# Hyena's long convolution on one NeuronCore: all elementwise steps between its transforms on VectorE, none on GpSimd

## The chip, the core and the metric

The kernel runs on one core of one Trainium2 chip. A core has five engines that run their own instruction streams and meet through semaphores: TensorE (PE in the profile; its weight loads are PEld), VectorE (DVE), ScalarE (ACT), GpSimd (POOL) and SyncE (SP, which here only issues DMAs). The metric is the device time of one execution in microseconds (us); lower is better.

## The reference

Two layers of a diffusion backbone over 128 context and 1024 latent tokens. Each layer projects the normed tokens into three groups that run side by side: a convolution module, attention with normed and rotated q and k, and a Hyena long convolution. Then follow an output projection and a gated FFN. The part that the change touches is the long convolution, twice per layer:

```
def _fft_conv(u, kf, bias):
    L = u.shape[1]
    U = jnp.fft.rfft(u, n=2 * L, axis=1)
    y = jnp.fft.irfft(U * kf[None], n=2 * L, axis=1)[:, :L]
    return y + u * bias
...
def _hyena(z, p):
    z = _dwconv(z, p['hy_short_w'], p['hy_short_b'])
    v, g1, g2 = jnp.split(z.astype(jnp.float32), 3, axis=-1)
    kf = _hyena_filter_fft(z.shape[1], p)
    bias = p['hy_bias'].astype(jnp.float32)
    u = _fft_conv(v, kf[:, 0], bias[0]) * g1
    u = _fft_conv(u, kf[:, 1], bias[1]) * g2
    return u.astype(z.dtype)
```

## The kernel before

All matrix work is in fp32 split into a high and a low part, so one product is three matmuls (`hh*whi`, `hl*whi`, `hh*wlo`). A layer has four phases; each is one loop, and a list scheduler puts every engine's instructions into one fixed order before the run.

Phase 1 (`phase1`) is the input projection: 16 output blocks, each of 72 matmuls (tile `win`; 2304 in both layers, 1152 in each). The weights of a block come as `wraw`; ScalarE makes the high part `whi`, GpSimd the low part `wlo`. After its matmuls a block is treated by its kind: blocks of the Hyena group go through a short convolution (`raw`, then `zs` on VectorE); q and k blocks through a norm and a rotation (TensorE sums `s` and broadcasts `nr`, VectorE's reciprocal `nsd`, its `nw` and `sh`, and GpSimd's two products with the rotary table); gates through `th`.

Between the matmuls of these blocks, the Hyena convolutions run as a background generator. `hy_conv` does one 2048-point convolution: four DFT matrix products (`ft`, read out into `ta` and `sd`), then elementwise butterflies (`e`, `p`, `o`, `abcd`, `jk`, `X`), the product with the filter's spectrum for four parts n (`W` and `Y`, from `X` and the loaded `khat`), butterflies back (`isd`, `s`, `d`, `e`, `f`, `vw`, `pqmn`, `gh`, `Z`), the split into `zh` and `zl`, and four inverse products (`iy`). The 128 context tokens take a small path of their own within it (`xp`, `pab`, `pyh`, `yp`, `yp2t`). It runs twice per layer; the second ends with transposes `y2t` and the products `hyo`, which are split into `mh` and `ml` and written to memory.

When the second convolution is done, its buffers are given to attention: keys `k` are loaded by GpSimd's DMA queue and queries `q` by SP's, and TensorE starts with the row maxima (`S`, reduced by VectorE into `mx`). Phase 2 is attention with the convolution module beside it; phases 3 and 4 are the output projection (`wo`) and the FFN (`up`, `dn`).

In `hy_conv`, `eng` is GpSimd. It does the 16 butterflies on 128x256 tiles (`abcd`, `jk`, `pqmn`, `gh`: four each) and the four 128x1024 products `W`; everything else elementwise in it is VectorE's.

Of the kernel before, what the change touches and what calls it, by code (L numbers as in the profile page):

```python
# [134 lines left out]
class Kern:  # L135
# [684 lines left out]
    def hy_conv(self, l, o, mid):  # L820

        nc = self.nc
        eng = nc.gpsimd

        def v2(x):
            return x.rearrange("p (c x) -> p c x", c=2)

        def sw(x):
            return v2(x)[:, ::-1, :]

        def v4(t):
            return t[:].rearrange("p (n x) -> p n x", n=4)

        def two(name):
            t = self.H(name)
            return t[:, 0:512], t[:, 512:1024]

        def part(F, n, r):
            t = self.T("ft")
            uh, ul = self.u[r]  # L840
            for c in range(2):
                j = 128 * (2 * n + c)
                self.mm3(t[:, 256 * c : 256 * c + 256], F[:, j : j + 128], F[:, 512 + j : 640 + j], uh, ul, True, True)
            return t

        def sd(q):
            F = self.hq.tile([128, 1024], F32R, tag="fm", name="fmat", bufs=2)
            self.const(F[:], "dftf", q)
            a = part(F, 0, q)
            m = self.M("ta")  # L850
            nc.scalar.copy(m[:], a[:])
            b = part(F, 1, q + 4)
            s, d = two("sd")
            self.add(s, m[:], b[:])
            self.sub(d, m[:], b[:])
            return s, d

        s0, d0 = sd(0)
        s2, d2 = sd(2)
        yield  # L860
        E0, E2 = two("e02")
        self.add(E0, s0, s2)
        self.sub(E2, s0, s2)
        P1, P3 = two("p13")
        self.add(v2(P1), v2(d0), sw(d2))
        self.sub(v2(P3), v2(d0), sw(d2))
        yield
        s1, d1 = sd(1)
        s3, d3 = sd(3)
        yield  # L870
        O0, O2 = two("o02")
        self.add(O0, s1, s3)
        self.sub(O2, s1, s3)
        t = self.H("abcd")
        A, C, B, D = (t[:, 256 * k : 256 * k + 256] for k in range(4))
        self.add(A, d1[:, 0:256], d1[:, 256:512], eng)
        self.sub(C, d1[:, 256:512], d1[:, 0:256], eng)
        self.sub(B, d3[:, 256:512], d3[:, 0:256], eng)
        self.add(D, d3[:, 0:256], d3[:, 256:512], eng)
        J, K_ = two("jk")  # L880
        self.add(J[:, 0:256], A, B, eng)
        self.sub(J[:, 256:512], B, A, eng)
        self.add(K_[:, 0:256], C, D, eng)
        self.sub(K_[:, 256:512], C, D, eng)
        yield
        Y = []
        for n in range(4):
            X = self.H("X")
            x = v4(X)
            if n == 0:  # L890
                self.add(x[:, 0:4:2, :], v2(E0), v2(O0))
                self.sub(x[:, 1:4:2, :], v2(E0), v2(O0))
            elif n == 1:
                self.add(x[:, 0:4:3, :], v2(E2), sw(O2))
                self.sub(x[:, 1:3, :], v2(E2), sw(O2))
            else:
                c = SQH if n == 2 else -SQH
                self.stt(x[:, 0:4:3, :], v2(J), c, v2(P1), ALU.mult, ALU.add)
                self.stt(x[:, 1:3, :], v2(K_), c, v2(P3), ALU.mult, ALU.add)
            K = self.hq.tile([128, 1024], F32, tag="kh", name="khat", bufs=2)  # L900
            nc.sync.dma_start(K[:], self.khD[l][o, n])

            def kb(c):
                return K[:, 512 * c : 512 * c + 512].unsqueeze(1).to_broadcast([128, 2, 512])

            y, w = self.H("Y"), self.H("W")
            self.mul(v2(w[:]), v2(X[:]), kb(1), eng)
            self.mul(v2(y[:]), v2(X[:]), kb(0))
            self.sub(y[:, 0:512], y[:, 0:512], w[:, 512:1024])
            self.add(y[:, 512:1024], y[:, 512:1024], w[:, 0:512])  # L910
            Y.append(y)
            yield
        mid()

        ds = []
        for n in range(2):
            s, d = two("isd")
            self.add(v2(s), v4(Y[n])[:, 0:4:2, :], v4(Y[n])[:, 1:4:2, :])
            self.sub(v2(d), v4(Y[n])[:, 0:4:2, :], v4(Y[n])[:, 1:4:2, :])
            ds.append((s, d))  # L920
        (s0, d0), (s2, d2) = ds
        S13, D13 = self.H("s13"), self.H("d13")
        self.add(S13[:], Y[2][:], Y[3][:])
        self.sub(D13[:], Y[2][:], Y[3][:])
        yield
        e0, e1 = two("e01")
        self.add(e0, s0, s2)
        self.sub(e1, s0, s2)
        f0, f1 = two("f01")
        s1, s3 = v4(S13)[:, 0:4:2, :], v4(S13)[:, 1:4:2, :]  # L930
        self.add(v2(f0), s1, s3)
        self.sub(v2(f1), s1, s3)

        V, W = two("vw")
        self.sub(v2(V), v2(d0), sw(d2))
        self.add(v2(W), v2(d0), sw(d2))
        t = self.H("pqmn")
        p_, q_, m_, n_ = (t[:, 256 * k : 256 * k + 256] for k in range(4))
        d = v4(D13)
        self.sub(p_, d[:, 0, :], d[:, 2, :], eng)  # L940
        self.add(q_, d[:, 0, :], d[:, 2, :], eng)
        self.add(m_, d[:, 1, :], d[:, 3, :], eng)
        self.sub(n_, d[:, 1, :], d[:, 3, :], eng)
        G, Hh = two("gh")
        self.sub(G[:, 0:256], p_, m_, eng)
        self.add(G[:, 256:512], p_, m_, eng)
        self.add(Hh[:, 0:256], q_, n_, eng)
        self.sub(Hh[:, 256:512], n_, q_, eng)
        yield
        for n in range(4):  # L950
            Z = self.H("Z")
            z = v4(Z)
            if n == 0:
                self.add(Z[:, 0:512], e0, f0)
                self.sub(Z[:, 512:1024], e0, f0)
            elif n == 1:

                self.add(z[:, 2:0:-1, :], v2(e1), sw(f1))
                self.sub(z[:, 0:4:3, :], v2(e1), sw(f1))
            else:  # L960
                c = SQH if n == 2 else -SQH
                self.stt(z[:, 0:4:3, :], v2(G), c, v2(V), ALU.mult, ALU.add)
                self.stt(z[:, 1:3, :], v2(Hh), c, sw(W), ALU.mult, ALU.add)
            zh, zl = self.H("zh", F32R), self.H("zl", F32R)
            self.hilo(zh[:], zl[:], Z[:])
            F = self.hq.tile([128, 1024], F32R, tag="fm", name="imat", bufs=2)
            self.const(F[:], "dfti", n)
            t = self.T("iy")
            for u in range(2):
                for c in range(2):  # L970
                    j = 2 * u + c
                    self.mm3(t[:, 256 * u : 256 * u + 256], F[:, 128 * j : 128 * j + 128], F[:, 512 + 128 * j : 640 + 128 * j],
                             zh[:, 256 * j : 256 * j + 256], zl[:, 256 * j : 256 * j + 256], c == 0, c == 1)
            yield n, t
# [896 lines left out]
```

## Time and profile before

| | |
|---|---|
| median of 3 runs | 3429.67 us (3425.01 to 3435.25) |
| the profiled execution: its time, its span | 3432.48 us, 3430.7 us |
| PE busy, share of the span | 3172.1 us, 92% |
| DVE | 2195.4 us, 64% |
| ACT | 1190.9 us, 35% |
| POOL | 725.4 us, 21% |
| mean granted clock of TensorE | 0.948 |

The time of an execution is 1.8 us more than its span, the stretch from its first instruction to its last. A busy share is a mean over phases that have different limits: what a step costs is read in its own stretch. A duration on DVE or POOL in this profile is the time from an instruction's start to its end, so a wait in the middle of one shows as a longer instruction and not as idle time. The granted clock is a share of TensorE's full 2.4 GHz.

### The profile page before, as it was taken

How to read it: one execution, taken by the hardware profiler on the slowest of the kernel's cores; microseconds unless marked ns; L12 is line 12 of the kernel's file. 1: busy time of each engine (PE TensorE's matmuls, PEld its weight loads, DVE VectorE, ACT ScalarE, POOL GpSimd, SP SyncE). 2: the span in 40 equal slices, each digit the busy share in tenths (PEclk: the TensorE clock that was granted, in tenths of full speed). 3: DMA queues.
4: the chain of work that ended last, by engine and by line, in shares of the span. 5: the costliest groups of instructions: out<-in, count | busy, mean ns of one | idle time of the engine just before them, and what ended most of it. 6: DMA issues, size and time to landing. Idle time of an engine off the chain costs nothing. (4 is left out here: it accounts for less than half of the span.)

```text
span 3430.7 us, 44677 instructions
## 1 busy us (share of the span) xinstructions
PE 3172.1 (92%) x17330; PEld 2794.1 (81%) x17330; DVE 2195.4 (64%) x3318; ACT 1190.9 (35%) x1976; POOL 725.4 (21%) x558
## 2 busy tenths in 40 slices
PE   5988878999889999999999889789999999999997
PEld 3878833458889999999998887334699999999997
DVE  7877789764764554445577795996446554455556
ACT  3422333352253222333344233334434223333323
POOL 6645444221210000000024562442101000000002
PEclk8989978999989999999999998889999999999998
DMA  7564454536311111111123535442511111111112
GB/s 285 163 206 155 129 154 140 173 114 222 122 53 41 44 42 42 44 42 42 44 70 112 163 114 157 141 148 79 191 41 37 44 44 41 44 43 41 44 42 70
DMA packets 152328, 336.09 MB, mean 98 GB/s; under 512 B 21360, under 2 KB 57844, under 8 KB 145589
## 3 DMA queue, kind: packets, MB, share of 16 engines
q1 hardware_dynamic: 147412, 318.69, 28.7%
q0 software_dynamic: 4704, 14.55, 1.5%
q8 instruction: 137, 2.24, 0.3%
q14 instruction: 75, 0.61, 0.1%
HBM read 264.86 MB, written 68.31 MB: 97 GB/s over the span
## 5 line engine op out<-in xcount | busy, mean ns | idle before, releaser
L236 PE MATMUL up<-hl,whi 128*128 128x384 f32 (+1 forms) x2112 | 713.7, 338 | 4.6 <-DVE hl L225 3.2
L236 PE MATMUL up<-hh,whi 128*128 128x384 f32 (+1 forms) x2112 | 711.7, 338 | 3.6 <-ACT hh L230 2.3
L236 PE MATMUL up<-hh,wlo 128*128 128x384 f32 (+1 forms) x2112 | 712.5, 338 | 0.0
L213 DVE TENSOR_TENSOR wlo<-wraw,whi 128x512 fp32r<-128x512 f32 x296 | 207.1, 700 | 646.5 <-ACT whi L230 644.2
L230 ACT CAST whi<-wraw 128x512 fp32r<-128x512 f32 x362 | 223.8, 618 | 845.1 <-PE dn L236 358.2
L236 PEld LDWEIGHTS up<-hl,whi 128*128 128x128 f32 x2112 | 399.5, 189 | 6.5 <-DVE hl L225 4.7
L236 PEld LDWEIGHTS up<-hh,whi 128*128 128x128 f32 x2112 | 399.5, 189 | 4.4 <-ACT hh L230 2.9
L236 PEld LDWEIGHTS up<-hh,wlo 128*128 128x128 f32 x2112 | 399.3, 189 | 0.0
L213 POOL TENSOR_TENSOR acc<-acc,sq 128x384 f32<-128x384 f32 x51 | 56.0, 1106 | 1623.4 <-ACT sq L210 1622.4
L225 DVE SCALAR_TENSOR_TENSOR xt<-dn,mod,xt 128x128 f32<-128x128 f32 (+2 forms) x704 | 332.0, 511 | 71.7 <-PE dn L236 71.5
L236 PE MATMUL dn<-gh,wlo 128*128 128x384 f32 (+1 forms) x1056 | 359.2, 340 | 0.0
L236 PE MATMUL dn<-gh,whi 128*128 128x384 f32 (+1 forms) x1056 | 358.2, 339 | 0.0
L236 PE MATMUL dn<-gl,whi 128*128 128x384 f32 (+1 forms) x1056 | 357.5, 339 | 0.0
L225 DVE SCALAR_TENSOR_TENSOR fu<-pd,vec,fu 128x1154 f32<-128x1154 f32 (+2 forms) x192 | 253.8, 1323 | 91.7 <-ACT fu L210 89.1
L236 PE MATMUL win<-hh,whi 128*128 128x384 f32 x768 | 270.4, 354 | 27.7 <-ACT raw L729 10.2
L236 PE MATMUL win<-hl,whi 128*128 128x384 f32 x768 | 269.4, 351 | 7.8 <-POOL hl L213 3.6
L236 PE MATMUL win<-hh,wlo 128*128 128x384 f32 x768 | 268.5, 350 | 1.2 <-POOL wlo L213 1.2
L1344 DVE TENSOR_REDUCE mx<-S 128x1 f32<-128x384 f32 x384 | 197.4, 547 | 66.3 <-PE S L236 65.8
L1665 ACT COPY pd<-up 128x384 f32<-128x384 f32 (+1 forms) x352 | 131.9, 401 | 237.7 <-PE up L236 237.7
L210 ACT ACTIVATE p<-st 128x1024 f32<-128x1024 f32 x144 | 147.0, 1021 | 166.9 <-PE st L236 166.5
L236 PEld LDWEIGHTS dn<-gl,whi 128*128 128x128 f32 x1056 | 200.0, 189 | 0.0
L236 PEld LDWEIGHTS S<-k,q 128*128 128x128 f32 x384 | 76.2, 218 | 151.8 <-DVE mx L1344 64.3
(295 smaller groups left out, 5675.6 us busy)
## 6 DMA issues: line engine op xcount, KB each, us to landing
wmod<-in_w_mod SPq DMA_DIRECT2D x48, 1024.0 KB
wraw<-in_w_up SPq DMA_DIRECT2D x176, 256.0 KB
wraw<-in_w_dn SPq DMA_DIRECT2D x88, 256.0 KB
wraw<-in_w_in SPq DMA_DIRECT2D x64, 256.0 KB
q<-qD SPq DMA_DIRECT2D x48, 256.0 KB
mh<-mixD SPq DMA_DIRECT2D x16, 576.0 KB
ml<-mixD SPq DMA_DIRECT2D x16, 576.0 KB
khD<-fK SPq DMA_DIRECT2D x16, 512.0 KB
```

The costliest lines, as they stand in the source:

```text
L210: return self.nc.scalar.activation(out, in_, f, **k)
L213: return (eng or self.nc.vector).tensor_tensor(out, a, b, op=op)
L225: return (eng or self.nc.vector).scalar_tensor_tensor(out, a, s, b, op0=op0, op1=op1)
L230: self.nc.scalar.copy(hi, src)
L236: self.nc.tensor.matmul(out, l, r, start=start, stop=stop)
L1344: nc.vector.tensor_reduce(m3[:, k, s : s + 1], S[:, :384], op=ALU.max, axis=AX.X)
L1665: self.nc.scalar.copy(p[:, u + o : v + o], t[:, u - a : v - a])
```

## The change

`eng` is taken out of `hy_conv`: the 20 instructions per convolution that GpSimd did are issued on VectorE, in the same program order, on the same tiles. With two convolutions in each of two layers these are 64 instructions on 128x256 and 16 on 128x1024.

```
 def hy_conv(self, l, o, mid):
-        eng = nc.gpsimd
...
-        self.add(A, d1[:, 0:256], d1[:, 256:512], eng)
-        self.sub(C, d1[:, 256:512], d1[:, 0:256], eng)
-        self.sub(B, d3[:, 256:512], d3[:, 0:256], eng)
-        self.add(D, d3[:, 0:256], d3[:, 256:512], eng)
+        self.add(A, d1[:, 0:256], d1[:, 256:512])
+        self.sub(C, d1[:, 256:512], d1[:, 0:256])
+        self.sub(B, d3[:, 256:512], d3[:, 0:256])
+        self.add(D, d3[:, 0:256], d3[:, 256:512])
...
-        self.add(J[:, 0:256], A, B, eng)
+        self.add(J[:, 0:256], A, B)
...
-            self.mul(v2(w[:]), v2(X[:]), kb(1), eng)
+            self.mul(v2(w[:]), v2(X[:]), kb(1))
...
-        self.sub(p_, d[:, 0, :], d[:, 2, :], eng)
+        self.sub(p_, d[:, 0, :], d[:, 2, :])
...
-        self.sub(G[:, 0:256], p_, m_, eng)
+        self.sub(G[:, 0:256], p_, m_)
...
```

The scheduler builds its order anew, so other instructions move too. On VectorE, in the first convolution of layer 0, these rows stood before, from the first `Y<-Y,W` (each row is an operation, its output and inputs, its size, and how many of it):

```order
L213 TENSOR_TENSOR Y<-Y,W 128x512 x2
L225 SCALAR_TENSOR_TENSOR X<-jk,p_1578 128x2x256
L225 SCALAR_TENSOR_TENSOR X<-jk,p_1578 128x512
L213 TENSOR_TENSOR Y<-Y,W 128x512 x2
L213 TENSOR_TENSOR Y<-X,khat 128x1024
L225 SCALAR_TENSOR_TENSOR X<-jk,p_1578 128x2x256
L225 SCALAR_TENSOR_TENSOR X<-jk,p_1578 128x512
L213 TENSOR_TENSOR Y<-Y,W 128x512 x2
L213 TENSOR_TENSOR Y<-X,khat 128x1024
L213 TENSOR_TENSOR pab<-xp,khatp 128x512 x2
L213 TENSOR_TENSOR Y<-Y,W 128x512 x2
L1076 RECIPROCAL nsd<-nsd 128x18
```

and these stand now, from the `zs` that comes ahead of the same `Y<-Y,W`:

```order
L225 SCALAR_TENSOR_TENSOR zs<-raw,vec_77,zs 128x1153
L213 TENSOR_TENSOR Y<-Y,W 128x512 x2
L213 TENSOR_TENSOR W<-X,khat 128x1024
L213 TENSOR_TENSOR Y<-X,khat 128x1024
L225 SCALAR_TENSOR_TENSOR X<-jk,p_1578 128x2x256
L225 SCALAR_TENSOR_TENSOR X<-jk,p_1578 128x512
L213 TENSOR_TENSOR Y<-Y,W 128x512 x2
L213 TENSOR_TENSOR W<-X,khat 128x1024
L213 TENSOR_TENSOR Y<-X,khat 128x1024
L225 SCALAR_TENSOR_TENSOR X<-jk,p_1578 128x2x256
L225 SCALAR_TENSOR_TENSOR X<-jk,p_1578 128x512
L1075 RECIPROCAL nsd<-nsd 128x18
```

`W` stands ahead of each `Y<-X,khat`, and the reciprocal `nsd` comes ahead of the third `Y<-Y,W`, where it came behind the fourth; two `zs` stand ahead of it in both orders. The same list has `abcd` and `jk` right behind `o<-sd`, some ten rows up.

On TensorE, at the end of layer 0's second convolution, the last transposes `y2t` were followed before by:

```order
L246 MATMUL y2t<-cst,y_3102 128x128 x4
L236 MATMUL win<-hh,wlo 128x384
L236 MATMUL s_3913<-cst,nsq 128x2 x9
L236 MATMUL win<-hh,whi 128x384
L236 MATMUL win<-hl,whi 128x384
L236 MATMUL win<-hh,wlo 128x384
L236 MATMUL win<-hh,whi 128x384
L236 MATMUL win<-hl,whi 128x384
```

and by 61 `win` matmuls in all ahead of the first `S`. Now there stands:

```order
L246 MATMUL y2t<-cst,y_3102 128x128 x4
L236 MATMUL nr<-cst,nsd 64x128 x6
L236 MATMUL s_4098<-cst,nsq 128x2 x9
L236 MATMUL nr<-cst,nsd 64x128 x18
L236 MATMUL sp<-kpt,qp 128x128 x2
L246 MATMUL ppt<-cst,pp 128x128 x2
L236 MATMUL avp<-ppm,vpt 64x128 x2
L236 MATMUL S<-k_3584,q_3599 128x384 x3
```

All 1152 `win` matmuls of the layer come ahead of the last `y2t`, and the last norms (`nr`, `s`) and a first piece of the context tokens' attention (`sp`, `ppt`, `avp`) ahead of `S`. In layer 1 the last `y2t` has moved back behind 73 more `win` (93 of them still follow it, where 166 did). Between `xp` and the first `yp` of layer 0's second convolution stand 203 `win`, where 157 did; of layer 1's second, 130 where 140 did. The first `iy` of layer 0 stands behind 648 of the `win`, where it stood behind 610; that of layer 1 behind 1716, where it stood behind 1668.

## Rows read from the trace of the kernel before

**Rows 1.** Busy time, granted clock and DMA of three stretches, by engine.

```profile
core 0: us, PE busy (x) PEld busy (x) DVE busy (x) ACT busy (x) POOL busy (x), PEclk, DMA share, GB/s
190.00:433.00 243.00, 205.86 (x1300) 196.99 (x1301) 192.64 (x237) 72.33 (x135) 117.82 (x104) 0.93 0.49 154
1040.00:1800.00 760.00, 757.04 (x4336) 756.40 (x4335) 408.93 (x611) 240.94 (x392) 19.55 (x18) 1.00 0.16 45
1870.00:2091.00 221.00, 194.44 (x1208) 188.25 (x1206) 170.43 (x212) 69.26 (x123) 125.70 (x94) 0.93 0.44 140
```

**Rows 2.** Timeline of TensorE: start, us, instruction, idle time before it and releaser.

```profile
248.81 1.55 PE L236 MATMUL nr<-cst,nsd 128*64 128x128 f32 x12 [11.71 <-DVE nsd L1076]
...
269.31 0.43 PE L236 MATMUL nr<-cst,nsd 128*64 128x128 f32 x2 [4.66 <-DVE nw L213]
...
346.20 0.69 PE L236 MATMUL win<-hh,whi 128*128 128x384 f32 x1 [5.68 <-ACT th L210]
...
382.35 0.33 PE L246 MATMUL yp2t<-cst,yp 128*128 128x128 f32 x1 [3.76 <-DVE hyo L213]
...
1910.92 0.69 PE L236 MATMUL win<-hh,whi 128*128 128x384 f32 x1 [10.17 <-ACT raw L729]
...
1931.30 0.39 PE L236 MATMUL iy<-zh,imat 128*128 128x256 f32 x1 [3.02 <-ACT zh L230]
...
2009.40 0.69 PE L236 MATMUL win<-hh,whi 128*128 128x384 f32 x1 [7.62 <-ACT nw L210]
```

**Rows 3.** Timeline of VectorE in layer 0's first convolution.

```profile
211.63 7.59 DVE L213 TENSOR_TENSOR o<-sd 128x512 f32<-128x512 f32 x2
...
248.68 0.68 DVE L213 TENSOR_TENSOR pab<-pab 128x256 f32<-128x256 f32 x2
```

**Rows 4.** Timeline of GpSimd at the first of these.

```profile
211.21 2.82 POOL L213 TENSOR_TENSOR abcd<-sd 128x256 f32<-128x256 f32 x4
...
216.64 1.42 POOL L213 TENSOR_TENSOR jk<-abcd 128x256 f32<-128x256 f32 x2
```

**Rows 5.** Instructions by tile, whole run: ns least/median/most, first and last start.

```profile
L213 DVE TENSOR_TENSOR Y<-Y,W x32: 674/1382/2894, 229.2 to 2021.2; 128x512 f32<-128x512 f32 x32
L213 DVE TENSOR_TENSOR Y<-X,khat x16: 1210/1346/3475, 220.5 to 2014.9; 128x1024 f32<-128x1024 f32 x16
L213 POOL TENSOR_TENSOR W<-X,khat x16: 2395/2689/3396, 220.5 to 2014.3; 128x1024 f32<-128x1024 f32 x16
L213 POOL TENSOR_TENSOR abcd<-sd x16: 726/750/1854, 211.2 to 1985.8; 128x256 f32<-128x256 f32 x16
```

**Rows 6.** GpSimd's low parts of weights, 190 to 433 us: busy, mean, idle before.

```profile
L213 POOL TENSOR_TENSOR wlo<-wraw,whi 128x512 fp32r<-128x512 f32 x21 | 32.7, 1557 | 57.3 <-ACT whi L230 57.3
```

**Rows 7.** Timeline of VectorE, layer 0's second convolution, last `sd` and `pyh`.

```profile
323.71 0.68 DVE L213 TENSOR_TENSOR sd<-ta,ft 128x512 f32<-128x512 f32 x1
...
368.53 0.68 DVE L213 TENSOR_TENSOR pyh<-pab,pyh 128x512 fp32r<-128x512 f32 x1
```

**Rows 8.** Timeline of VectorE in layer 1: first convolution, then the second.

```profile
1873.49 1.90 DVE L213 TENSOR_TENSOR o<-sd 128x512 f32<-128x512 f32 x2
...
1908.81 1.41 DVE L225 SCALAR_TENSOR_TENSOR zs<-raw,vec,zs 128x1153 f32<-128x1153 f32 x1
...
1983.51 1.28 DVE L213 TENSOR_TENSOR sd<-ta,ft 128x512 f32<-128x512 f32 x2 [2.34 <-PE ft L236]
...
2024.90 0.68 DVE L213 TENSOR_TENSOR pyh<-pab,pyh 128x512 fp32r<-128x512 f32 x1
```

**Rows 9.** TensorE's last transposes of each layer (by tile), and the first `S`.

```profile
L246 PE MATMUL y2t<-cst,y x16: 272/273/273, 391.4 to 409.5; 128*128 128x128 f32 x16
...
432.82 1.30 PE L236 MATMUL S<-k,q 128*128 128x384 f32 x3 [4.41 <-DMA q<-qD]
...
L246 PE MATMUL y2t<-cst,y x16: 270/273/473, 2047.0 to 2068.9; 128*128 128x128 f32 x16
...
2090.98 0.77 PE L236 MATMUL S<-k,q 128*128 128x384 f32 x3 [1.80 <-DMA q<-qD]
```

More of the change, by code (lines that the diff above doesn't have):

```diff
@@ L875, in hy_conv @@
         A, C, B, D = (t[:, 256 * k : 256 * k + 256] for k in range(4))
-        self.add(A, d1[:, 0:256], d1[:, 256:512], eng)
-        self.sub(C, d1[:, 256:512], d1[:, 0:256], eng)
-        self.sub(B, d3[:, 256:512], d3[:, 0:256], eng)
-        self.add(D, d3[:, 0:256], d3[:, 256:512], eng)
+        self.add(A, d1[:, 0:256], d1[:, 256:512])
+        self.sub(C, d1[:, 256:512], d1[:, 0:256])
+        self.sub(B, d3[:, 256:512], d3[:, 0:256])
+        self.add(D, d3[:, 0:256], d3[:, 256:512])
         J, K_ = two("jk")
-        self.add(J[:, 0:256], A, B, eng)
-        self.sub(J[:, 256:512], B, A, eng)
-        self.add(K_[:, 0:256], C, D, eng)
-        self.sub(K_[:, 256:512], C, D, eng)
+        self.add(J[:, 0:256], A, B)
+        self.sub(J[:, 256:512], B, A)
+        self.add(K_[:, 0:256], C, D)
+        self.sub(K_[:, 256:512], C, D)
         yield
@@ L939, in hy_conv @@
         d = v4(D13)
-        self.sub(p_, d[:, 0, :], d[:, 2, :], eng)
-        self.add(q_, d[:, 0, :], d[:, 2, :], eng)
-        self.add(m_, d[:, 1, :], d[:, 3, :], eng)
-        self.sub(n_, d[:, 1, :], d[:, 3, :], eng)
+        self.sub(p_, d[:, 0, :], d[:, 2, :])
+        self.add(q_, d[:, 0, :], d[:, 2, :])
+        self.add(m_, d[:, 1, :], d[:, 3, :])
+        self.sub(n_, d[:, 1, :], d[:, 3, :])
         G, Hh = two("gh")
-        self.sub(G[:, 0:256], p_, m_, eng)
-        self.add(G[:, 256:512], p_, m_, eng)
-        self.add(Hh[:, 0:256], q_, n_, eng)
-        self.sub(Hh[:, 256:512], n_, q_, eng)
+        self.sub(G[:, 0:256], p_, m_)
+        self.add(G[:, 256:512], p_, m_)
+        self.add(Hh[:, 0:256], q_, n_)
+        self.sub(Hh[:, 256:512], n_, q_)
         yield
```

## Prediction

> **What bounds the kernel now.** I read the busy time by stretch first. Over the FFN (1040 to 1800 us) TensorE is busy for 757 of 760 us at a granted clock of 1.00, the level of 2.4 GHz; nothing this change touches works there. The convolutions run in phase 1 of each layer, 190 to 433 us and 1870 to 2091 us, and there TensorE is idle for 37.1 and 26.6 us and its clock is 0.93 [rows 1]. VectorE is busy for 79% and 77% of these stretches. So the change is worth what it does to TensorE's waits there.
>
> Second, the timeline of TensorE, for its idle times with what ended them. The seven long ones are 11.71, 4.66, 5.68 and 3.76 us in layer 0 and 10.17, 3.02 and 7.62 us in layer 1 [rows 2], 46.6 of the 63.7 us. Each ends with VectorE or with a ScalarE step that hangs on VectorE (`raw` on the previous block's `zs`, `nw` and `th` on buffers that VectorE's rotation steps free, `zh` on `Z`).
>
> Third, the timelines of VectorE and GpSimd side by side, for why VectorE is late. Two `o<-sd` take 7.59 us from 211.63 [rows 3], where a `Y<-Y,W` of the same size can take 0.674 [rows 5]. In that time GpSimd works from 211.21 to 218.06 without a pause, `abcd` to `jk` [rows 4], and VectorE is through at 219.2, some 1.2 us later. The median `Y<-Y,W` takes 1.38 us, twice its least [rows 5]. Here one of the two stands still while the other works.
>
> The Trainium skill, "SBUF — State Buffer", section "Who interferes with whom", has this as a rule: a VectorE instruction with two inputs in SBUF contends with a GpSimd instruction that reads SBUF, the one that issued first holds the shared port for the whole instruction, and the other blocks. The trace agrees (7.59 us for work of 1.35). Taken in full it would give VectorE back all that GpSimd no longer does; that is the third rival below.
>
> **The change, part by part.** *Work.* GpSimd loses 16 `W` of 2.69 us at the median, 43.0 us, and 64 small ones of at least 0.726, 46.5 us: 89 us at least [rows 5]. VectorE gets 16 products of the form of `Y<-X,khat`, 1.21 us when nothing holds it up [rows 5], and 64 of 128x256, 0.34 each by the pair of `pab` at 0.68 [rows 3]: 19.4 + 21.8 = 41 us, 10.3 per convolution. Which of TensorE's waits this moves is worked out chain by chain. I add the instructions of the new order at their least (0.674 for 128x512, 1.21, 0.34, and 1.41 for `zs` [rows 8]; 0.5 for the small ones of the rotation, between these), and 1.56 us for each `wlo` that GpSimd still does in the stretch [rows 6], as if every one stopped VectorE.
>
> *Layer 0, first convolution.* Before, TensorE stood from 237.1 to 248.8 until the reciprocal `nsd` was done, 37.2 us after VectorE's 211.63 [rows 2, 3]. Now 14 of 128x512, 6 of 1024, 8 small ones and 2 `zs` stand ahead of it: 9.4 + 7.3 + 2.7 + 2.8 = 22.2, and two `wlo` 3.1, which is 236.9. The wait goes, and I count 11 of its 11.71 us; bounds 8.6 (both `wlo` twice as long) and 11.71. Of the next, 4.66 at `nr`, I take 2: the first `iy`, 38 `win` later in the order (6.7 us at 757.04/4336 = 0.175 each [rows 1]), becomes the place that waits for `Z`. Bounds 0 and 4.66.
>
> *Layer 0, second convolution.* From the last `sd` (ends 324.4) to `pyh` (369.2) VectorE took 44.8 us [rows 7]. The new list is 25 of 512, 8 of 1024, 10 small and 14 of the rotation, 16.9 + 9.7 + 3.4 + 7.0 = 37.0, and three `wlo`: 41.7. TensorE has 203 `win`, 35.5 us, and 2 us of `nr` to do meanwhile, so 4 us of waiting remain at `yp`, where 5.68 and the smaller ones at `yp` stood; and `yp2t`, which waited 3.76, has 29 `win` (5 us) ahead of it. I take 8 us; bounds 3 (the chain's own gain) and 9.4 (both waits).
>
> *Layer 1, first convolution.* The `zs` that freed `raw` was through at 1910.2, 36.7 us after 1873.49 [rows 8]; TensorE had stood since 1900.7 [rows 2]. Now 12 of 512, 6 of 1024, 8 small and 4 `zs` lead to it: 8.1 + 7.3 + 2.7 + 5.6 = 23.7, and two `wlo`: 1900.3. Of 10.17 us 9 go, and the 3.02 at `iy`, behind 48 more `win` (8.4 us), too: 12. Bounds 6 and 13.2.
>
> *Layer 1, second convolution.* From the end of `sd` at 1984.8 to that of `pyh` at 2025.6 it took 40.8 us [rows 8]. The new list is 16.9 + 9.7 + 3.4 + 5.0 and three `wlo`, 39.7; TensorE has 130 `win` and some 4 us of small matmuls, 27 us. The 7.62 us wait becomes one at `yp`: I take the chain's gain, 1 us. Bounds -8 and 7.6.
>
> *The tails.* Attention can start only when the last `hyo` is out. From the last `y2t` to the first `S` it took 23.3 us (409.5 to 432.8) and 22.1 us (2068.9 to 2091.0), and both ended with the load of `q` [rows 9]. In layer 0 that was covered by 61 `win` (10.7 us), which now come first; nothing covers it now but 27 `nr` and a piece of the context's attention. In layer 1 the last `y2t` comes 73 `win` (12.8 us) later. What came out of the cover is done earlier, so nothing is lost where VectorE and the loads set the pace behind `S`, and all of it where TensorE does. I take a loss of 2 us each; bounds 0 and 23.5 together.
>
> *The clock.* 0.93 against 1.00 [rows 1]: one point is worth 4.0 us of the 400 us busy in the two stretches. It fell where TensorE had stood. I take one point, 4 us; bounds 0 and 28.
>
> *What GpSimd keeps.* Its rotation products also stop VectorE, which the lists leave out: 4 us against, bounds 0 and 10.
>
> Edits that cost nothing: GpSimd's own queue gets shorter, which hides behind its waits for `whi` (57.3 us idle ahead of 21 `wlo` [rows 6]); the `khat` loads have to follow faster, but two buffers give them the 7 us that VectorE needs from one `Y<-X,khat` to the `W` two parts on (X, two `Y<-Y,W`, `W`, `Y`, X, two `Y<-Y,W`, by the prices above). If they don't land, each part waits for its load.
>
> Sum: 11 + 2 + 8 + 12 + 1 + 4 - 4 - 4 = 30 us. The profiled execution took 3432.48 us, 2.8 above the median of the runs, so 3402.5 for one like it and 3399.7 by the median: **3400 us**.
>
> **The rivals.** *No change.* The tails take it back: the chains give 14 + 3 + 10 + 1 = 28 us and the covers taken away are worth 23.5, which leaves 4.5: 3425. For it: TensorE's total work is the same, and layer 0's end stands bare. Against: in both layers the start of `S` was set by loads, not by TensorE [rows 9].
>
> *Slower.* VectorE becomes the bound: `wlo` and the rotation go on holding it, it gains no speed, and 10.3 us more lie in each of the four chains. Where half of that reaches TensorE it is 20 us, 3450; in full 41, 3471. It decides if the median `Y<-Y,W` stays above 1 us. For it: VectorE is already busy for 79% [rows 1], and the 89 us go to the busier engine. Against: the least and the median of the same instruction [rows 5]. The Trainium skill, "Perfetto Trace Analysis", section "Optimizing Scalar/DVE Operations", speaks for this side where it advises to move work off a saturated VectorE, to ScalarE or even GpSimd; the same section warns that between VectorE and GpSimd it might not help, because they share a read port, and by the rows above the trace sides with the warning.
>
> *More than forecast.* Every microsecond of GpSimd's 89 had stopped VectorE, so VectorE is relieved by 48 net, all seven waits go (46.6) and the clock gives another 8: 55, or 3375. Against: in the second convolutions the counted chains hardly get shorter.
>
> **How the numbers follow.** A difference of 0.3%, 10 us, is what a measurement here can tell from no change. Chances: the forecast (a gain of 11 to 45 us) 0.68, more than that 0.07, no change 0.13, slower 0.12. So faster 0.75, same 0.13, slower 0.12. The range runs from just beyond the third rival's 3375 to 3438, where the slower rival begins; it leaves out some 0.16. The forecast's own range is 3385 to 3419.
>
> **What would show it.** Right: `Y<-Y,W` at a median near 0.7 us and `o<-sd` at 1.3 for two; the 11.71 and the 10.17 us waits gone; a wait of some 10 us at `yp` in layer 1; some 20 us of TensorE idling between the last `y2t` and `S` in layer 0. Wrong: `Y<-Y,W` still above 1 us, `S` starting later than 432.8 us, TensorE waiting for `wlo` (held up by long runs of VectorE) or VectorE for `khat`.

## The result and the profile after

The changed kernel takes 3379.84 us, the median of four runs (3374.35 to 3384.74), where the kernel before took 3431.21 beside it: a ratio of 0.985, interval 0.9834 to 0.9865, or 51 us less. The forecast was 3400. The result lies inside the prediction's whole range (3375 to 3438), but 5 us below the forecast's own (3385 to 3419) and 5 us above the third rival's 3375.

The profiled execution has a span of 3372.2 us, the shortest of the four runs, against 3430.7; the accounts below are of this pair and add up to 58.5 us. Of these, 46.1 are TensorE's idle time (258.6 to 212.5) and 12.4 its busy time (3172.1 to 3159.7).

First the windows of each layer's convolutions, the stretch from the last `y2t` to the first `S`, and attention up to the first `wo`. Before:

```profile
core 0: us, PE busy (x) PEld busy (x) DVE busy (x) ACT busy (x) POOL busy (x), PEclk, DMA share, GB/s
190.00:409.50 219.50, 187.84 (x1165) 180.32 (x1166) 183.08 (x215) 63.85 (x118) 108.89 (x92) 0.93 0.45 145
409.50:432.80 23.30, 17.84 (x136) 16.47 (x135) 9.56 (x22) 8.47 (x17) 8.93 (x12) 0.95 0.83 238
432.80:786.30 353.50, 309.69 (x1360) 149.47 (x1360) 276.26 (x479) 144.05 (x206) 120.15 (x64) 0.88 0.46 154
...
1800.00:2068.90 268.90, 236.94 (x1440) 226.95 (x1439) 210.72 (x264) 95.59 (x176) 144.37 (x117) 0.93 0.40 128
2068.90:2090.98 22.08, 20.28 (x125) 20.22 (x123) 6.98 (x14) 8.72 (x16) 7.62 (x10) 1.00 0.77 238
2090.98:2456.90 365.92, 317.75 (x1410) 162.33 (x1410) 286.90 (x484) 148.34 (x215) 122.14 (x67) 0.88 0.40 130
```

The same stretches after (layer 1's begins again at the end of the FFN):

```profile
190.00:392.90 202.90, 196.20 (x1268) 189.31 (x1269) 173.15 (x266) 72.13 (x130) 62.54 (x55) 0.97 0.52 166
392.90:420.60 27.70, 11.15 (x80) 8.17 (x78) 15.25 (x40) 9.07 (x21) 14.61 (x21) 0.58 0.83 229
420.60:754.00 333.40, 297.91 (x1299) 142.51 (x1299) 259.99 (x448) 138.65 (x193) 109.76 (x53) 0.89 0.47 158
...
1766.10:2022.90 256.80, 244.12 (x1512) 234.40 (x1511) 203.49 (x306) 97.34 (x180) 101.25 (x81) 0.97 0.42 139
2022.90:2047.90 25.00, 22.02 (x139) 21.11 (x138) 7.47 (x17) 9.21 (x18) 5.62 (x9) 0.93 0.84 241
2047.90:2400.50 352.60, 307.93 (x1323) 150.44 (x1321) 282.67 (x478) 145.69 (x210) 120.17 (x65) 0.87 0.40 130
```

Idle time of TensorE is the length less the first busy time. In the convolutions it falls from 31.66 to 6.70 and from 31.96 to 12.68 us: 44.2 in all. In layer 0's tail it rises from 5.46 to 16.55, in layer 1's from 1.80 to 2.98: 12.3 lost. In the attention phases it falls by 8.3 and 3.5: 11.8. In layer 0's convolutions VectorE is busy for 173 us where it was for 183, with more work.

Some of the idle times of TensorE that are left there, the two longest among them (timeline of the kernel after; in brackets the idle time before the row and what ended it), against [rows 2]:

```profile
250.22 0.86 PE L236 MATMUL yp<-pyh,pmat 128*128 128x256 f32 x5 [1.37 <-DVE pyh L213]
...
353.58 0.38 PE L236 MATMUL yp<-pyh,pmat 128*128 128x256 f32 x1 [1.75 <-ACT pyh L230]
...
1970.50 0.44 PE L236 MATMUL win<-hh,whi 128*128 128x384 f32 x1 [2.90 <-DVE th L225]
...
1997.20 0.38 PE L236 MATMUL iy<-zh,imat 128*128 128x256 f32 x1 [1.04 <-ACT zh L230]
```

At none of the places of the seven long ones is more left than these 2.90 us. VectorE's timeline at the start of that first one, against [rows 3], and at the end of layer 1's second, against [rows 8]:

```profile
212.53 1.29 DVE L213 TENSOR_TENSOR o<-sd 128x512 f32<-128x512 f32 x2
213.74 1.42 DVE L213 TENSOR_TENSOR abcd<-sd 128x256 f32<-128x256 f32 x4
...
236.35 0.25 DVE L1075 RECIPROCAL nsd<-nsd 128x18 f32<-128x18 f32 x1
...
1941.65 1.29 DVE L213 TENSOR_TENSOR sd<-ta,ft 128x512 f32<-128x512 f32 x2 [1.17 <-PE vt L246]
...
1978.35 0.68 DVE L213 TENSOR_TENSOR pyh<-pab,pyh 128x512 fp32r<-128x512 f32 x1
```

Two `o<-sd` take 1.29 us where they took 7.59, and the reciprocal is through 24.1 us after their start instead of 37.2. By tile (ns least/median/most), against [rows 5]:

```profile
L213 DVE TENSOR_TENSOR Y<-Y,W x32: 621/680/1780, 225.9 to 1972.1; 128x512 f32<-128x512 f32 x32
L213 DVE TENSOR_TENSOR Y<-X,khat x16: 1208/1214/2311, 221.2 to 1967.6; 128x1024 f32<-128x1024 f32 x16
L213 DVE TENSOR_TENSOR W<-X,khat x16: 1208/1213/2034, 220.1 to 1966.4; 128x1024 f32<-128x1024 f32 x16
L213 DVE TENSOR_TENSOR abcd<-sd x16: 411/418/422, 213.7 to 1945.7; 128x256 f32<-128x256 f32 x16
```

The 80 moved instructions are busy for 51.0 us on VectorE (20.9 for `W`; 5.9, 7.1, 8.3 and 8.8 for `abcd`, `jk`, `pqmn` and `gh`), and yet its busy time falls from 2195.4 to 2166.0 us: what it had to do before takes 80 us less, nearly all of the 89 that GpSimd's work was at its least (GpSimd was busy with it for 111 us). GpSimd's own busy time falls by less than that, by 98.6 us (725.4 to 626.8): its `wlo` now take 128.1 us in all, where they took 110.5.

Attention's first rows in TensorE's timeline, against [rows 9] (`issue` is idle time in which the profile shows nothing that the engine waited for):

```profile
420.59 1.30 PE L236 MATMUL S<-k,q 128*128 128x384 f32 x3 [4.82 <-issue]
...
2047.87 0.70 PE L236 MATMUL S<-k,q 128*128 128x384 f32 x3
```

### The profile page after: what moved, and what is told of

The parts are those of the page before. It is cut to its first block, busy times and chain, and to the rows that moved or that the text cites. A ratio compares the mean times of both kernels' runs of the same rounds, so it can differ in the third digit from the quotient of the medians.

```text
span 3372.2 us, 44662 instructions
## 1 busy us (share of the span) xinstructions
PE 3159.7 (94%) x17330; PEld 2782.6 (83%) x17330; DVE 2166.0 (64%) x3398; ACT 1193.9 (35%) x1978; POOL 626.8 (19%) x478
## 4 chain that ended last, share of the span: by engine, by line
PE 72%; DVE 17%; DMA 6%; issue 2%; ACT 1%; POOL 1%; SPq 1%; DVEq 0%; ACTq 0%; POOLq 0%
PE up L236 32%; PE dn L236 16%; PE win L236 6%; PE wo L236 6%; DVE ca L225 3%; PE av L236 2%; PE st L236 2%; DVE mx L1343 2%; PE S L236 2%; DVE nt L225 1%; DMA q<-qD 1%; DVE Y L213 1%; PE fc L236 1%; DVE hl L225 1%; PE flt L236 1%
## 5 line engine op out<-in xcount | busy, mean ns | idle before, releaser
L225 DVE SCALAR_TENSOR_TENSOR xt<-dn,mod,xt 128x128 f32<-128x128 f32 (+2 forms) x704 | 332.3, 513 | 71.7 <-PE dn L236 71.5
L236 PEld LDWEIGHTS dn<-gh,whi 128*128 128x128 f32 x1056 | 199.7, 189 | 0.0
```

What stands on the lines that cost most here:

```text
L225: return (eng or self.nc.vector).scalar_tensor_tensor(out, a, s, b, op0=op0, op1=op1)
L236: self.nc.tensor.matmul(out, l, r, start=start, stop=stop)
```

## The experiments

Theory A: VectorE's instructions with two operands in SBUF stand still while GpSimd reads its own, so the work that leaves GpSimd gives VectorE its time back. Theory B: nothing stands still; GpSimd is only the slower engine in the chain (2.69 us for a `W` against 1.21), and the chain gets shorter. The table has all runs; the columns behind the interval are of the profiled execution.

| run | median, us | ratio to before, interval | TensorE busy | TensorE idle | VectorE busy |
|---|---|---|---|---|---|
| before | 3431.21 | | 3172.1 | 258.6 | 2195.4 |
| after | 3379.84 | 0.985, 0.9834 to 0.9865 | 3159.7 | 212.5 | 2166.0 |
| w_only | 3397.43 | 0.9896, 0.9878 to 0.9913 | 3161.0 | 230.4 | 2179.4 |
| small_only | 3395.62 | 0.989, 0.9872 to 0.9909 | 3159.3 | 238.4 | 2186.7 |
| layer0_only | 3391.88 | 0.9883, 0.9863 to 0.9903 | 3163.6 | 233.6 | 2177.2 |
| layer1_only | 3409.52 | 0.993, 0.9913 to 0.9948 | 3163.2 | 243.9 | 2177.2 |
| gp_reads | 3420.32 | 0.9962, 0.995 to 0.9975 | 3161.1 | 261.5 | 2206.7 |
| gp_writes | 3383.51 | 0.9865, 0.9845 to 0.9885 | 3161.5 | 220.0 | 2166.5 |
| rope_too | 3366.73 | 0.9808, 0.9789 to 0.9827 | 3150.0 | 213.7 | 2179.3 |
| wlo_too | 3353.02 | 0.9768, 0.9747 to 0.9789 | 3148.8 | 202.5 | 2158.1 |
| rope_wlo | 3342.76 | 0.9728, 0.9709 to 0.9746 | 3140.0 | 204.3 | 2174.1 |
| rope_wlo_es | 3333.65 | 0.9707, 0.9687 to 0.9727 | 3135.5 | 197.4 | 2186.1 |
| rope_wlo_filt | 3346.02 | 0.974, 0.9725 to 0.9755 | 3145.4 | 200.3 | 2176.1 |
| rope_wlo_es_cz | 3342.54 | 0.9737, 0.9718 to 0.9756 | 3144.1 | 198.0 | 2182.7 |

### Parts of the change: w_only, small_only, layer0_only, layer1_only

Each takes `eng` out of one part alone:

```
w_only       self.mul(v2(w[:]), v2(X[:]), kb(1))             the 16 small ones keep eng
small_only   self.mul(v2(w[:]), v2(X[:]), kb(1), nc.gpsimd)  the 16 small ones on VectorE
layer0_only  eng = nc.gpsimd if l == 1 else None             all 20
layer1_only  eng = nc.gpsimd if l == 0 else None             all 20
```

> Only the four products W of each convolution go to VectorE; the 16 butterflies on 128x256 stay on GpSimd. Theory A (while GpSimd reads its operands VectorE's instruction stands still): the median Y<-Y,W falls from 1.38 to near 0.68 us, because nothing of GpSimd's lies beside it any more but the rotation and the low parts of weights, while o<-sd next to abcd keeps some of its length (7.59 for two in the worst case before, 1.3 without GpSimd). W is 43 of the 111 us that GpSimd was busy with these steps, so about 40% of the 51 us: 3410 us. Theory B (nothing stands still, the chain is shorter only because VectorE does a step in less time than GpSimd): Y<-Y,W stays above 1.2 us, and 16 x (2.69 - 1.21) = 24 us at most, some of it covered: 3415 to 3425.

> Only the 16 butterflies on 128x256 of each convolution go to VectorE; the four W stay on GpSimd. Theory A: two o<-sd take near 1.3 us everywhere, Y<-Y,W keeps its median of 1.3 to 1.4, and about 60% of the 51 us come: 3400 us. With the run that moves W alone the gains add up to that of the whole change within some 10 us. Theory B: o<-sd stays long beside nothing, Y<-Y,W too, and 64 x (0.73 - 0.34) = 25 us at most: 3410 to 3425.

> The whole change in layer 0 alone; in layer 1 the order of TensorE is that of before. Theory A with the accounts of the two traces: layer 0 (to its first wo) gave 32 of 58 us, so about 28 of the 51: 3403 us, with the first S at 421 us and the first wo of layer 0 at 754; layer 1 as long as before. By the prediction's terms layer 0 gives 11 + 2 + 8 - 2 and half of the rest, 19: 3412. Rival: the gain of one layer is given back or enlarged by the other (the clock or loads carry over), and the two parts do not add up to 51.

> The whole change in layer 1 alone. Theory A with the accounts of the two traces: layer 1 gave some 24 of 58 us, so about 21 of the 51: 3410 us. By the prediction's terms layer 1 gives 12 + 1 - 2 and half of the rest, 11: 3420. Rival: as for layer 0, the parts do not add up.

Measured against the 3435.08 us of the kernel before beside them: 38, 39, 43 and 26 us faster. Three came in faster than theory A had it (3397 against 3410, 3396 against 3400, 3392 against 3403), the fourth as it had it (3410). The halves by kind add up to 77 us, those by layer to 69, and the whole is 51: my expectation of adding up failed. Part of the excess lies in the difference of executions: the profiled ones gain 39.3 and 33.0 us by kind, 72 together, and 33.5 and 23.6 by layer, 57, where that of the whole gains 58.5. For these the two columns of TensorE say where it comes from. Idle time roughly adds up: `w_only` loses 28.2 us of it and `small_only` 20.2, 48 together against 46 for the whole; the layers lose 25.0 and 14.7, 40. Busy time does not: it is 9 to 13 us less in each part, and 12 less in the whole. By layer one sees the place: from layer 1's first `win` to its first `wo` TensorE is busy for 576.9 us before, for 569.4 in `layer1_only`, and again for 576.9 in the changed kernel. Why, these runs don't say.

In `w_only` the median `Y<-Y,W` is 0.679 us, and one `o<-sd` beside GpSimd's `abcd` still takes up to 6.98 us. In `small_only` `o<-sd` takes 0.684 at the median (0.687 at most). Both are as theory A has it. But the median `Y<-Y,W` of `small_only` fell to 0.686, too, though GpSimd kept `W` and I had expected 1.3 to 1.4 (by tile, ns least/median/most):

```profile
L213 DVE TENSOR_TENSOR Y<-Y,W x32: 622/686/2896, 228.9 to 2000.7; 128x512 f32<-128x512 f32 x32
L213 POOL TENSOR_TENSOR W<-X,khat x16: 2339/2702/6959, 221.2 to 1993.5; 128x1024 f32<-128x1024 f32 x16
```

The stalls are still there: 21 of the 32 lie beside a `W`, and 15 take 1.2 to 2.9 us, where 17 did before. The median falls into the gap between the short and the long ones, and two instructions moved it across. One `W` of GpSimd's, on the other side, takes 6.96 us. A median alone therefore does not tell the theories apart.

### Reading or only being busy: gp_reads, gp_writes

The changed kernel, with GpSimd given idle work whose result nobody uses, at the places of the steps that it lost (each run has one of the two bodies of `dup`):

```
+        scr = self.hq.tile([128, 896], F32, tag="scr", name="scr", bufs=1)
+        def dup(n):
+            self.add(scr[:, 0:n], self.cs[:, 0:n], self.cs[:, 1024 : 1024 + n], nc.gpsimd)   # gp_reads
+            for k in range(3 if n == 896 else 1):                                            # gp_writes
+                nc.gpsimd.memset(scr[:, 0 : 880 if n == 896 else 768], 0.0)
...
+        for _ in range(8):            # behind jk, and behind gh
+            dup(256)
...
+            dup(896)                  # behind each W
```

> The whole change, and beside it GpSimd does, at the same places of each convolution, four additions on 128x896 and 16 on 128x256 of two pieces of the rotary table into a scratch tile that nobody reads: some 84 us of reading (16 x 2.35 + 64 x 0.73) on which nothing depends. VectorE's work is that of the changed kernel. Theory A (VectorE stands still while GpSimd reads): VectorE's instructions grow again where the two lie side by side, its busy time by 40 to 80 us, and the time goes back most of the way: 3405 to 3430 us. Theory B (only the chain's latency counted): 3375 to 3385, as the changed kernel.

> As the run before, but GpSimd fills the scratch tile with zeros instead (three fills of 880 columns for each product, one of 768 for each small step, by 1.05 us for 1152 columns some 84 us too): just as long on GpSimd, with no operand read. The order of TensorE is that of the changed kernel. Theory A: within 8 us of the changed kernel, 3375 to 3390. If it is GpSimd's own queue that counts (the low parts of weights come late behind the new work), it is as slow as the run with the additions. If writing alone holds VectorE up, too; the two would then be told apart by VectorE's durations.

The additions kept GpSimd busy for 103.8 us, the fills for 87.5. With the fills the kernel takes 3383.51 us, 4 more than the changed kernel, which is less than can be told, and VectorE is busy for 2166.5 us as there. With the additions it takes 3420.32, 40 more: VectorE's busy time rises by 40.2 us against `gp_writes`, TensorE's idle time by 41.5, its busy time by nothing. So each of the 103.8 us of reading cost VectorE 0.4 us. VectorE's timeline at the first butterflies of layer 0, with the fills and with the additions beside it:

```profile
201.01 1.29 DVE L213 TENSOR_TENSOR e<-sd 128x512 f32<-128x512 f32 x2
```

```profile
198.65 1.28 DVE L213 TENSOR_TENSOR sd<-ta,ft 128x512 f32<-128x512 f32 x2 [0.49 <-PE ft L236]
199.85 4.26 DVE L213 TENSOR_TENSOR e<-sd 128x512 f32<-128x512 f32 x2
204.04 4.53 DVE L213 TENSOR_TENSOR p<-sd 128x512 f32<-128x512 f32 x2
```

GpSimd's timeline in the same stretch, of gp_writes and then of gp_reads:

```profile
200.52 5.23 POOL L827 MEMSET scr<- 128x880 f32 x6
```

```profile
197.65 2.13 POOL L213 TENSOR_TENSOR scr<-cs 128x896 f32<-128x896 f32 x1
199.72 1.31 POOL L213 TENSOR_TENSOR wlo<-wraw,whi 128x512 fp32r<-128x512 f32 x1
200.97 2.60 POOL L213 TENSOR_TENSOR scr<-cs 128x896 f32<-128x896 f32 x1
...
204.72 4.43 POOL L213 TENSOR_TENSOR scr<-cs 128x896 f32<-128x896 f32 x3
```

The pair `e` ends at 204.1 and `p` at 208.6, where 1.3 us for each pair would do. `sd`, which takes its second operand from PSUM, is not held up (1.28 us beside an addition). The price reaches TensorE, first of all at the place where it stood longest before the change, in gp_reads' timeline:

```profile
257.97 1.55 PE L236 MATMUL nr<-cst,nsd 128*64 128x128 f32 x12 [16.27 <-DVE nsd L1084]
```

In the whole run TensorE waits once for a `wlo`, for 0.5 us, so GpSimd's fuller queue is not the cause. Nothing depends on these additions, so theory B falls: it had 3375 to 3385. One reserve: the scheduler put some instructions of gp_reads elsewhere (in layer 0, 458 `win` ahead of the first `xp`, and not 441). In gp_writes the order is that of the changed kernel throughout layer 0, but the traces show TensorE's order differing in some places of layer 1, which I had not expected. The Trainium skill, "SBUF — State Buffer", section "Who interferes with whom", draws the line at the same place: GpSimd instructions that read SBUF contend with VectorE's of two SBUF inputs, not those that only write it. The trace agrees, with 1.29 us for the pair `e` beside the fills and 4.26 beside a `wlo` and an addition.

### Further off GpSimd: rope_too, wlo_too, rope_wlo

```
 def rope_out            nc, g = self.nc, None             (was self.nc.gpsimd; rope_too, rope_wlo)
 def phase1              self.wl_eng = None                (was nc.gpsimd; wlo_too, rope_wlo)
```

> The whole change, and the two products of the rotation (60 instructions, 65.6 us on GpSimd before) on VectorE as well. Theory A: VectorE takes some 60 x 0.5 = 30 us of work and is relieved of part of the 66; GpSimd no longer stands in the chain to the queries: 3370 to 3380 us. Rival: in the second convolutions VectorE is the one that TensorE waits for, and 15 us more per layer on it come out at yp and at the start of S: 3390 to 3400.

> The whole change, and the low parts of the input projection's weights (64 instructions of 1.68 us on GpSimd) on VectorE as well, 0.68 us each. Theory A: VectorE gets 43 us of work and is relieved of up to 107 us of holds: 3365 to 3375. Rival: a weight now waits in VectorE's queue behind the convolution's long runs, and TensorE waits for it: 3385 to 3400.

> The whole change, and both the products of the rotation and the low parts of the input projection's weights on VectorE: in the projection phase GpSimd has no arithmetic left. If the two steps add up (13 and 27 us against the changed kernel): 3340 us. Rival: with everything on VectorE it is the end of the convolutions that sets the start of attention, both layers' ends stand bare, and the second step gives only what the first left: 3348 to 3355.

They are 13, 27 and 37 us below the changed kernel. The first two did better than theory A's own ranges, by 3 and 12 us, and together they nearly add up (3343 where 3340 was expected). In wlo_too VectorE's busy time falls by another 8 us (2166.0 to 2158.1) though it takes over 66 instructions, and TensorE waits nowhere for a `wlo`. The rivals of all three runs fall. But that these gains come by TensorE waiting less is shown in part only: in the profiled executions `rope_too` has as much idle time as the changed kernel (213.7 against 212.5) and is faster by TensorE's busy time (3150.0 against 3159.7), and of the 28 us that `rope_wlo` gains 8 are idle time and 20 busy time, for which these runs show no cause.

### Where the rule ends: rope_wlo_es, rope_wlo_filt, rope_wlo_es_cz

```
 rope_wlo_es     self.add(part[k][:], held[k][:] if c < 4 else part[k][:], P[:])    es, attention
 rope_wlo_filt   yield from self.filt_one(l, o, None)                               the filter
 rope_wlo_es_cz  rope_wlo_es and self.add(Z[:], Z[:], y[:])                         cz, convolution module
```

> As the run with both steps, and in attention the 62 additions of the exponentials that GpSimd did (128x1024, 2.38 us at the median) are VectorE's, too, 1.21 us each: 75 us more for an engine that is busy for 91% of the first 146 us of that phase. The theory that VectorE stands still while GpSimd reads holds for its steps with two operands in SBUF; half of VectorE's time there is TENSOR_REDUCE, which takes 0.55 us beside an es of GpSimd's, too. So little is given back, and VectorE becomes the bound: 10 to 40 us slower than the run with both steps. Rival: the rule is general, every microsecond of GpSimd's costs one of VectorE's, and it is faster by 10 to 40 us.

> As the run with both steps, and the filter's butterflies (30 us of GpSimd's in the first 190 us, as much again beside layer 0's FFN, 128x512) on VectorE at 0.68 us each. In the first 190 us TensorE is idle for 44 us and VectorE busy for 144. By theory A it gets 5 to 15 us faster than the run with both steps, from the first 190 us alone; rival: those idle times belong to loads (the DMA share there is 0.66) and nothing moves.

> As rope_wlo_es, and the 36 additions cz of the convolution module (128x584, 1.83 us at the median on GpSimd) on VectorE at 0.76 us each: 27 us more, all in the stretch in which VectorE is busiest. My expectation for the additions of the exponentials failed: VectorE's busy time in layer 0's attention phase rose by 3.4 us where 39 were added, and the run was 9 us faster. If the rule is general (what GpSimd reads beside VectorE costs VectorE as much), the first half of the phase ends 5 to 15 us sooner in each layer: 3315 to 3330. The rival, that VectorE is the bound of the first half and gets nothing back there: TensorE's idle time in the two phases, 68.6 us, grows by 10 to 27 and it takes 3345 to 3360.

`rope_wlo_es` went against my expectation of a loss: 9 us faster, 3333.65, with intervals that just overlap. VectorE's additions `es` of layer 0 take 68.6 us instead of 30.5, yet its busy time in that attention phase is 266.8 instead of 263.4: some 35 us came back, among others from the taps `ca`. Their rows by tile (ns least/median/most) of rope_wlo, then of rope_wlo_es:

```profile
L225 DVE SCALAR_TENSOR_TENSOR ca<-cd,cwh,ca x60: 767/817/2955, 469.1 to 2216.0; 128x584 f32<-128x584 f32 x60
```

```profile
L225 DVE SCALAR_TENSOR_TENSOR ca<-cd,cwh,ca x60: 775/821/845, 472.7 to 2198.5; 128x584 f32<-128x584 f32 x60
```

I had argued from the medians, which were short already; the stalls sat in the few long ones. With `cz` moved as well, VectorE's busy time there stays at 266.3 us and TensorE's idle time in the two phases at 71.7 (68.6 before): neither the gain nor the loss that I had named. The time, 3342.54, is between the two expected ranges, and its interval overlaps that of rope_wlo_es. So the stalls that GpSimd's `cz` had caused went, and the work that replaced them on VectorE is about as long; TensorE's idle time stayed with VectorE's busy time. Whether TensorE still waits for VectorE there, this run doesn't tell. The filter's step moved nothing measurable (3346.02 against 3342.76); its rival stands as to the time. `rope_wlo_es` is the fastest version run, 100 us below the kernel before in the same comparison; from `rope_wlo` it can hardly be told.

## Why the prediction was right, and where its size was off

**What bounds.** Right: the seven waits hung on VectorE, and VectorE was late because GpSimd read beside it. gp_reads brings VectorE's stalls back and with them the first wait, as 16.27 us; the other six return only as shorter ones, in layer 0's convolutions 28.8 us of idle time in all, where gp_writes has 5.5.

**The work.** The 41 us that VectorE should get were 51: `W` at 1.30 in the mean, the small ones at 0.42 to 0.59 each where the pair of `pab` had suggested 0.34.

**The convolutions.** The terms came to 11 + 2 + 8 + 12 + 1 = 34 us, the idle time fell by 44.2 (25.0 and 19.3, against 21 and 13). The chains were counted well: 24.1 us to the reciprocal in layer 0's first, where my list came to 25.3 with its two `wlo`. Where the sum was too small is layer 1's second convolution, the step with "I take the chain's gain, 1 us": the wait of some 10 us at `yp` never came. The chain from `sd` to `pyh` took 36.1 us (39.7 counted), and beside it TensorE had 31 us of its own work, not 27: from `xp` at 1943.42 to the first `yp` at 1977.06 it idled only for the 2.90 us shown above. Beyond the seven waits, shorter ones went too.

**The tails.** Right that some 20 us would lie bare in layer 0: 16.55 us, and over both layers 12.3 more than before, where I had taken 4. (The cover that I counted as 27 `nr` is 24 `nr` and 9 `s` in the order shown.) But attention's idle time fell by 11.8, which no term held. In layer 0 it goes with the new order: `layer1_only` has before's order there, on every engine, and idles for 43.7 us in attention as before does (43.8); `layer0_only` and `gp_writes` have the changed kernel's and idle for 38.7 and 34.7 (35.5). So 5 to 9 us there are a consequence of the change by way of the scheduler, with some 4 us from one execution to the next; which wait they come from was not followed. In layer 1 no run repeats an order, and attention idles for 42 to 53 us in the kernels of the table down to `gp_writes`; the 3.5 us there can't be told from that.

**The clock.** One point, 4 us, was too little. The granted clock of the convolutions rose from 0.93 to 0.97 in both layers, and TensorE's busy time fell by 12.4 us, 10.1 of it from 190 us to layer 0's first `wo`. By the price of 4.0 us a point the four points would be 16. But the clock of the convolutions is not the whole of it: in layer 1 it rose as much, and the busy time of the three stretches shown fell by 0.9 us only (575.0 to 574.1), with the clock of the tail and of attention lower than before (0.93 against 1.00, 0.87 against 0.88).

**What GpSimd keeps.** The 4 us against were not to be seen as a term of their own; my lists had charged each `wlo` already. What the rest of GpSimd's work in the projection costs is measured, net of what the same steps take on VectorE: 37 us for the rotation and the low parts.

**The rivals.** "No change" falls: the time is 51 us shorter, and the tails took 12 us, not 23.5. (The chains that it counted, 14 + 3 + 10 + 1 us, are not those of the parts, 13, 8, 12 and 1, and the prediction doesn't say why.) "Slower" falls by the point that it named, a median `Y<-Y,W` of 0.680 us. The Trainium skill's advice in "Perfetto Trace Analysis", section "Optimizing Scalar/DVE Operations", to relieve a saturated VectorE is not what this case tests (VectorE was busy for 77 to 79% there); the warning in the same section, that moving work between VectorE and GpSimd might not help, agrees with the 51 us that taking it back gave. "More than forecast" came nearest: of its mechanism 80 of 89 us were given back, and of the seven waits 2.90 us at most is left at one place. I gave it 0.07 on the ground that the counted chains of the second convolutions hardly get shorter. They got 3.8 and 4.7 us shorter (44.8 to 41.0, with 41.7 counted; 40.8 to 36.1, with 39.7), and TensorE's own work hid them.

So the sum missed by 28 us of the profiled pair's 58.5: 10 in the convolutions, 8 in TensorE's busy time (the term of the clock), 4 in the tails with attention, 4 in GpSimd's rest, 2 elsewhere. Between the medians it missed by 21; the other 7 are that the profiled execution of the changed kernel is the shortest of its four, and that of the kernel before is not.

## What to carry to other kernels

An elementwise step on GpSimd that reads SBUF is not free beside a VectorE that is busy with steps of two operands in SBUF: here 89 us of GpSimd's work cost VectorE 80 us, more than the 51 that the same steps take on VectorE itself. The price is not fixed: the 104 us of additions in gp_reads cost it 40. Look for instructions of one form whose most is several times their least, and set the two engines' timelines side by side; the median can hide it. What a further step is worth has to be run: the low parts gave 27 us, `cz` and the filter nothing that could be told.

## What the runs showed of the hardware that was not expected

GpSimd is held up as well, and the hold can outlast one instruction by far. In the changed kernel one `wlo` stands for 11.58 us where 1.26 will do (by tile before, then after, and its row in GpSimd's timeline):

```profile
L213 POOL TENSOR_TENSOR wlo<-wraw,whi x66: 1261/1301/7673, 40.1 to 2081.8; 128x512 fp32r<-128x512 f32 x66
```

```profile
L213 POOL TENSOR_TENSOR wlo<-wraw,whi x66: 1260/1463/11579, 40.4 to 2020.8; 128x512 fp32r<-128x512 f32 x66
...
1844.69 11.58 POOL L213 TENSOR_TENSOR wlo<-wraw,whi 128x512 fp32r<-128x512 f32 x1 [6.07 <-ACT whi L230]
```

In that time VectorE works without a pause, on steps with two operands in SBUF; it first stops at 1855.1, and the `wlo` is through 1.2 us later:

```profile
1853.82 1.29 DVE L225 SCALAR_TENSOR_TENSOR X<-jk,p 128x512 f32<-128x512 f32 x2
1857.77 1.42 DVE L225 SCALAR_TENSOR_TENSOR zs<-raw,vec,zs 128x1153 f32<-128x1153 f32 x1 [2.65 <-ACT zs L210]
```

It is the mirror image of [rows 3, 4], where VectorE stood until GpSimd's run was over at 218.06. So in these two places the engine that came second stood for the other's whole run and not for one instruction.

Also, in gp_reads GpSimd's additions of 128x256 between 190 and 442 us took 1.10 us in the mean, where the shortest of the run took 0.717; the 112 fills of gp_writes stayed between 730 and 859 ns. And TensorE's busy time for the same matmuls differs between the kernels by 37 us (3172.1 to 3135.5), a third of the whole gain of the fastest one. It doesn't follow the idle time: gp_reads idles for 3 us more than before and is busy for 11 less. The mean granted clock goes with it roughly (0.948 before, 0.952 after, 0.958 in rope_wlo); what sets it apart from the waits stays open.
